# A two-layer hybrid trunk: earlier decays, later masks, softmax scaled on another engine, other durations in the order's model

## The chip, the cores and the metric

One core of a Trainium2 chip runs the whole kernel. The metric is the device time of one execution in microseconds (us). The core's engines each work through a queue of their own in order and wait for each other by semaphores: TensorE (PE) multiplies matrices (PEld is its loading of weights), VectorE (DVE), ScalarE (ACT) and GpSimd (POOL) do the element-wise work, and DMA queues (SP issues most, POOL some) move data.

## The reference

Sequence 256, width 1024, two layers. Each layer is a SwiGLU half-step, a token mixing and a second half-step, each modulated by vectors computed from `c`:

```python
    for l in range(DEPTH):
        mod = c_act @ w_ada[l] + b_ada[l]
        sh1, sc1, gt1, sh2, sc2, gt2, sh3, sc3, gt3 = jnp.split(mod, N_MOD, axis=-1)
        h = modulate(x, ln_ffn1_g[l], sh1, sc1)
        x = x + 0.5 * gt1[:, None, :] * swiglu(h, ffn1_w_gate[l], ffn1_w_up[l], ffn1_w_down[l])
        h = modulate(x, ln_mix_g[l], sh2, sc2)
        x = x + gt2[:, None, :] * token_mixing(h, w_in[l], ...)
        h = modulate(x, ln_ffn2_g[l], sh3, sc3)
        x = x + 0.5 * gt3[:, None, :] * swiglu(h, ffn2_w_gate[l], ffn2_w_up[l], ffn2_w_down[l])
    return rmsnorm(x, final_g)
```

The mixing projects `h` once and gives the columns to three groups, whose outputs are joined and projected back:

```python
    # convolution: GLU, 31 causal taps per channel, LayerNorm, swish
    h = a * jax.nn.sigmoid(gate)
    h = causal_depthwise_conv(h, w_dw) + b_dw
    ...
    # attention (6 heads of 64): softmax over the causal scores, times the values
    p = jax.nn.softmax(jnp.concatenate([s_sel, s_own], axis=-1), axis=-1)
    ...
    # gated delta net (6 heads): short convolution and silu on q, k, v; then per chunk
    g = -jnp.exp(gdn_a_log) * jax.nn.softplus(a + gdn_dt_bias);  beta = jax.nn.sigmoid(b)
    g = jnp.cumsum(g)
    decay = jnp.exp(jnp.where(tril, g[..., :, None] - g[..., None, :], -jnp.inf))
    L = jnp.where(strict, jnp.einsum('bhncd,bhnsd->bhncs', k_beta, k) * decay, 0.0)
    T = lax.linalg.triangular_solve(eye + L, eye, left_side=True, lower=True)
    ...
    # then the state recurrence over the chunks, a gated RMSNorm and silu(z)
```

## The kernel before

The sequence lies in two halves of 128 rows. Weights are split into a high and a low part (`hi` cast on ACT, `lo` subtracted on DVE), and each product of the feed-forward parts and of most of the mixing is made of three matmuls. The phases follow each other: feed-forward, mixing, feed-forward, in each of two layers. The modulation vectors of the coming phases are added up on DVE meanwhile (`adaacc`, `Lb<-raw,c_act`), then summed on PE into bank `px` and reduced to `mod`.

Nobody writes the order of the mixing's instructions out by hand. While the program is built, a class `Clock` keeps a modelled time for each engine and adds `cost(engine, op, ...)` for every instruction. The mixing's side jobs are generators (`sides`): `key_norms`, `query_norms`, `decays`, `pairs`, `gate_conv`, `values_beta`, `inverse`, `delta_rule`, `attention`, two `taps` and `convolution`. Between two products of the main projection, `tick()` steps each generator whose awaited tiles are ready on the modelled clock, or whose named events (`until("kh")`) have been set. On the chip nothing of that model is left but the order in which each engine's instructions stand.

The names that count here. `pm<-Y,raw` are the first, unsplit products of the mixing's projection, `pm<-H,hi` and `pm<-H,lo` the split ones after it, `pm<-hi,H` those of the attention's values. `decays()` makes the exponentials of the decays: `g_g` holds the gates, `pa<-g_g,gt` sums them on PE, `Lb<-kc,g_r` and `S6a<-kc,g_r` spread them on DVE, `PT` takes the exponentials on ACT. `pairs()` multiplies the key products by `PT` into `xin_LT` (called `LD` in the code) and stores its 32x32 diagonal blocks to DRAM (`scr_l`). `inverse()` reads them back as 16x16 blocks (`Lb`), inverts these by 15 steps of two POOL operations (`T<-W,Lb`, `W<-W,T`; "the substitution"), stores the inverses (`scr_w`), reads them back (`Wc`) and joins the blocks on PE (`pa<-Wc,Lb`, `pa<-Lb,Wc` and further steps), the first of them with the off-diagonal blocks `Um` that POOL masks by `Lb<-xin_LT,kc`. `delta_rule()` needs the result. `attention()` makes, for a head, the scores on PE, the row maximum (`mx`) on DVE, the exponential and its sum (`E`, `sm`) on ACT, the reciprocal of the sum on DVE, the scaling of `E` by it, and the transposes `pa<-kc,E` on PE (`turned`), which are copied to `F` and multiplied by the values `V`. A tap of the convolution (`tap`) is either one DVE operation on `cacc`, or a product on ACT into `ctap`, of which there are two buffers, and an addition on POOL (`cacc<-cacc,ctap`); `taps` chooses by the modelled clocks. `closing` ends the mixing and prepares the next phase. All engine calls pass through one helper, so the profile gives the line L171 for each, and a reader goes by the names of the tiles.

Of the kernel before, what the change touches and what calls it, by code (L numbers as in the profile page):

```python
# [13 lines left out]
AF = mybir.ActivationFunctionType  # L14
OP = mybir.AluOpType
# [64 lines left out]
class Clock:  # L80
# [36 lines left out]
    def cost(self, engine, op, out, ins):  # L117
        n = max(self.size(x) for x in [out] + ins[:1])
        if engine == "pe":
            m, n, kind = self.size(ins[0]), self.size(ins[1]), ins[1].dtype  # L120
            if op == "transpose":
                return 0.107
            rows = 4 * max(m, n) if kind == F32 else max(2 * m, n) if kind == F32R else max(64, n)
            return 0.0065 + rows * 0.000435
        if engine == "act":
            return 0.1 + n * 0.00082 if n > 400 else 0.1 + n * 0.0011
        if engine == "gp":
            return max(0.17, 0.08 + n * 0.00222)
        if op == "reciprocal":
            return 0.07 + n * 0.0063  # L130
        return 0.11 + n * 0.00113 if op == "scalar_tensor_tensor" else 0.13 + n * 0.00105
# [46 lines left out]
def trunk(ctx, tc, t, out):  # L178
# [5 lines left out]
    act, dve, pe, gp, sp, qd = (clock.engine(n, e) for n, e in (  # L184
        ("act", nc.scalar), ("dve", nc.vector), ("pe", nc.tensor), ("gp", nc.gpsimd), ("dma", nc.sync), ("dma2", nc.gpsimd)))
# [27 lines left out]
    K = {n: kc[:, o:o + {"tri": 256, "rc": 256, "rs": 256, "eye": 32, "off": 32}.get(n, 128)] for n, o in K_OFF.items() if o < K_RES}  # L213
# [796 lines left out]
    def mixing(l, G, normed, nxt):  # L1010
# [4 lines left out]
        ev = {}  # L1015
# [42 lines left out]
        def until(*names):  # L1058
            while any(n not in ev for n in names):
                yield  # L1060
# [78 lines left out]
        LD = LT[:, :NH * 256].rearrange("p (h t x) -> p h t x", t=2, x=128)  # L1139
# [37 lines left out]
        def key_norms():  # L1177
            yield from until("kconv")

            def back():  # L1180
                act.preload_act_table_set("natural_log_exp_and_others")
                yield from ()

            yield from norms((kh[:, 0:2], kh[:, 2:3]), lambda: act.preload_act_table_set("silu_and_others"), back, 1.0)
            ev["kh"] = True
# [9 lines left out]
            ev["qh"] = True  # L1195

        def decays():
            yield from until("g", "kh")
            g, lnbeta = ev["g"], ev["lnbeta"]
            while any(job[1].tensor.name.startswith("Lb") for job in ada_wait):  # L1200
                extract()
            g, heads = g
            Rs = [sb([128, 1024], tag, F32R).rearrange("p (s k i x) -> p s k i x", s=2, k=2, i=2) for tag in ("Lb", "S6a")]
            cross = sb([128, NH], "g_c")

            def spread(b):
                dve.tensor_tensor(Rs[b % 2].rearrange("p s k i x -> p (s k i) x"), K["tri"][:, 0:128].unsqueeze(1).to_broadcast([128, 8, 128]),
                                  heads[:, 2 * b:2 * b + 2].rearrange("p h k i -> p (h k i)").unsqueeze(2).to_broadcast([128, 8, 128]),
                                  op=OP.mult)

            spread(0)
            spread(1)
            yield from room()
            p = pside([128, NH])
            mm(p, gt.bitcast(F32), g[:, 0], True)
            dve.tensor_tensor(cross, p, lnbeta[:, 0, NH:], op=OP.add)
            for b in range(3):
                R = Rs[b % 2]
                yield (R,)
                yield from room(2)  # L1220
                d = pside([128, 2, 2, 128], True)
                x = pside([128, 2, 128], True)
                for k in range(2):
                    mm(d, gt, R[:, :, k], k == 0, False)
                mm(d, identb, negdb.unsqueeze(1).to_broadcast([128, 4, 128]), False, True)
                for k in range(2):
                    mm(x, onesr, R[:, :, k, 1], k == 0, k == 1)
                if b == 0:
                    spread(2)
                yield (x,)  # L1230
                let_go(d)
                let_go(x)
                for s in range(2):
                    h = 2 * b + s
                    act.activation(PT[:, h, 0:128], d[:, s, 0], AF.Exp, bias=lnbeta[:, 0, NH + h:NH + h + 1])
                    act.activation(PT[:, h, 128:256], x[:, s], AF.Exp, bias=cross[:, h:h + 1])
                    act.activation(PT[:, h, 256:384], d[:, s, 1], AF.Exp, bias=lnbeta[:, 1, NH + h:NH + h + 1])
                    ev["decay", h] = True
            act.preload_act_table_set("silu_and_others")
            ev["silu2"] = True  # L1240

# [125 lines left out]
        def inverse():  # L1367
# [8 lines left out]
            for i in range(2):  # L1376
                c = slice(16 * i, 16 * i + 16)
                qd.dma_start(out=Lb[48 * i:48 * i + 48], in_=scr_l.rearrange("h b j i -> (h b) j i")[:, c, c])
            yield (LD,)
            LM = LD.rearrange("p h t x -> p (h t) x")  # L1380
            for q in QUAD:
                gp.tensor_tensor(Um[q], LM[q, :, q], K["off"][q].unsqueeze(1).to_broadcast([32, 12, 32]), op=OP.mult)
            yield (Lb, W)
            V = W[:, 0]
            for j in range(15):
# [10 lines left out]
            for f in range(2):  # L1396
                for i in range(2):
                    c = slice(16 * i, 16 * i + 16)
                    qd.dma_start(out=scr_w[f].rearrange("h b c i -> (h b) c i")[:, c, c], in_=W[48 * i:48 * i + 48, f])
            for f in (1, 0):  # L1400
                qd.dma_start(out=C[:, f], in_=scr_w[f].rearrange("h b c i -> (b c) h i"))
            yield from until("kh")
# [170 lines left out]
        def attention():  # L1573
# [14 lines left out]
            def softmax(h, p):  # L1588
                yield soon(p)
                mx = sb([128, 2], "mx", bufs=3)  # L1590
                sm = sb([128, 2], "sm", bufs=3)
                P = sb([128, 384], "E", bufs=3)
                for i, c in enumerate(cols):
                    dve.tensor_reduce(mx[:, i:i + 1], p[:, c], axis=AX.X, op=OP.max)
                dve.tensor_scalar(mx, mx, -0.125, None, op0=OP.mult)
                yield (mx,)
                for i, c in enumerate(cols):
                    act.activation(P[:, c], p[:, c], AF.Exp, scale=0.125, bias=mx[:, i:i + 1], accum_out=sm[:, i:i + 1])
                let_go(p)
                yield (sm,)  # L1600
                dve.reciprocal(sm, sm)
                yield (sm,)
                for i, c in enumerate(cols):
                    act.activation(P[:, c], P[:, c], AF.Copy, scale=sm[:, i:i + 1])
                Ps[h] = P
                ev["P", h] = P
                if len(Ps) and h == NH - 1:
                    ev["softmaxed"] = True
# [382 lines left out]
```

## Time and profile before

| what | value |
|---|---|
| time, three runs | 1204.75, 1204.11, 1202.5 us (median 1204.11) |
| the profiled execution: its time, its span | 1202.57 us, 1200.8 us |
| PE, PEld | 1130.7 us (94%), 1052.0 (88%) |
| DVE | 874.4 us (73%) |
| ACT | 612.6 us (51%) |
| POOL | 169.3 us (14%) |
| chain that ended last | PE 71%, DVE 12%, ACT 6%, POOL 6%, issue 3% |
| mean granted TensorE clock | 0.976 |

The span runs from the first to the last instruction of the profiled execution. A share of busy time is an average over phases: the mixings lie at about 235 to 435 us and 817 to 1004 us, the feed-forward parts fill the rest. [...]

### The profile page before, as it was taken

To read this page: it belongs to the slowest core of one execution; us is meant where nothing else is said; L and a number is where in the kernel's file an instruction comes from. 1 tells how busy PE (TensorE), PEld (TensorE's weight loads), DVE (VectorE), ACT (ScalarE), POOL (GpSimd) and SP (SyncE) were. 2 spreads that over 40 slices of the span, in tenths; PEclk is the share of its full clock that TensorE was granted. 3 is DMA by queue.
4 is the path that set the end of the run, shared out by engine and by line. 5 is a ranking of instruction groups with operands and counts; after the bars stand their busy time and mean duration, and the time that the engine had idled before them with its cause. 6 is when DMAs were issued, how large, how long until landed. Compare 5 with 4: busy or idle time off the path is not lost.

```text
span 1200.8 us, 22053 instructions
## 1 busy us (share of the span) xinstructions
PE 1130.7 (94%) x9085; PEld 1052.0 (88%) x9085; DVE 874.4 (73%) x1314; ACT 612.6 (51%) x1049; POOL 169.3 (14%) x213
## 2 busy tenths in 40 slices
PE   5799999999978789999999999999997899999997
PEld 4799999977767789999999999997876789999996
DVE  5778878757965788877778878774886759866554
ACT  4364443548367464434456544444654667544443
POOL 0610000011761010000000000001067401000001
PEclk9899999999999989999999999999999799999999
DMA  8759888836342558969865987892642334876640
GB/s 320 246 186 319 309 299 309 256 113 192 95 137 91 176 176 285 322 243 326 291 218 170 324 313 266 278 300 74 186 140 73 141 108 140 287 257 211 195 139 36
DMA packets 167661, 256.52 MB, mean 214 GB/s; under 512 B 8272, under 2 KB 134056, under 8 KB 167560
## 3 DMA queue, kind: packets, MB, share of 16 engines
q1 hardware_dynamic: 166536, 252.95, 62.6%
q0 software_dynamic: 1024, 2.16, 0.9%
q8 instruction: 71, 1.16, 0.4%
q14 instruction: 30, 0.25, 0.1%
HBM read 252.86 MB, written 2.23 MB: 212 GB/s over the span
## 4 chain that ended last, share of the span: by engine, by line
PE 71%; DVE 12%; ACT 6%; POOL 6%; issue 3%; DMA 1%; SPq 0%; POOLq 0%; DVEq 0%; ACTq 0%
PE pm L171 45%; PE pa L171 25%; DVE lo L171 3%; DVE adaacc L171 3%; PE px L171 2%; ACT hi L171 1%; POOL W L171 1%; POOL cacc L171 1%; POOL T L171 1%; POOL Lb L171 1%; DVE mod L171 1%; ACT L171 1%; DVE tmp L171 1%; DVE Lb L171 1%; DVE Y L171 1%
## 5 line engine op out<-in xcount | busy, mean ns | idle before, releaser
L171 PE MATMUL pm<-H,hi 128*128 128x256 f32 x2816 | 507.7, 283 | 2.8 <-issue 1.6
L171 DVE TENSOR_TENSOR lo<-raw,hi 128x1024 fp32r<-128x1024 f32 (+1 forms) x300 | 362.1, 1226 | 131.8 <-ACT hi L171 131.3
L171 PEld LDWEIGHTS pm<-H,hi 128*128 128x128 f32 x2816 | 431.9, 189 | 5.9 <-issue 2.2
L171 ACT CAST hi<-raw 128x1024 fp32r<-128x1024 f32 (+1 forms) x306 | 311.3, 1040 | 195.3 <-PE pm L171 80.7
L171 PE MATMUL pm<-H,lo 128*128 128x256 f32 x1408 | 392.4, 280 | 1.2 <-DVE lo L171 1.2
L171 PEld LDWEIGHTS pm<-H,lo 128*128 128x128 f32 x1408 | 264.5, 189 | 1.7 <-DVE lo L171 1.6
L171 PE MATMUL pa<-Y,hi 128*128 128x256 f32 x1312 | 241.3, 286 | 4.5 <-DVE xT L171 4.5
L171 PEld LDWEIGHTS pa<-Y,hi 128*128 128x128 f32 x1312 | 204.1, 192 | 6.7 <-DVE xT L171 5.3
L171 PE MATMUL pa<-Y,lo 128*128 128x256 f32 x656 | 185.8, 283 | 0.0
L171 PEld LDWEIGHTS pa<-Y,lo 128*128 128x128 f32 x656 | 127.3, 194 | 0.0
L171 POOL TENSOR_TENSOR xin_LT<-xin_LT 128x256 f32<-128x256 f32 x35 | 27.1, 775 | 664.8 <-ACT xin_LT L171 662.4
L171 ACT CAST Y<-tmp 128x256 fp32r<-128x256 f32 x88 | 35.8, 406 | 131.5 <-DVE tmp L171 131.5
L171 DVE SCALAR_TENSOR_TENSOR adaacc<-raw,c_act,adaacc 128x1024 f32<-128x1024 f32 x70 | 95.5, 1365 | 1.6
L171 DVE SCALAR_TENSOR_TENSOR Lb<-raw,c_act,Lb 128x1024 f32<-128x1024 f32 x56 | 71.8, 1283 | 4.2 <-DMA raw<-in_w_ada_dram 3.0
L171 POOL TENSOR_TENSOR cacc<-cacc,ctap 128x256 f32<-128x256 f32 x54 | 52.3, 973 | 122.0 <-DVE cacc L171 112.8
L171 DVE TENSOR_TENSOR Y<-tmp,Y 128x256 fp32r<-128x256 f32 x88 | 37.4, 425 | 41.5 <-ACT Y L171 41.5
L171 PE MATMUL pm<-Y,raw 128*128 128x256 f32 x288 | 66.8, 384 | 0.0
L171 PEld LDWEIGHTS pm<-Y,raw 128*128 128x128 f32 x288 | 53.4, 190 | 8.9 <-issue 1.0
L171 PE MATMUL pa<-hi,Y 128*128 128x512 f32 x176 | 54.8, 393 | 0.0
L171 ACT ACTIVATE tmp<-pm 128x256 f32<-128x256 f32 x84 | 31.8, 378 | 43.9 <-PE pm L171 43.7
L171 DVE TENSOR_REDUCE mod<-px 128x4 f32<-128x512 f32 x34 | 23.4, 689 | 34.3 <-PE px L171 34.2
L171 DVE SCALAR_TENSOR_TENSOR cacc<-hc,colB,cacc 128x256 f32<-128x256 f32 x66 | 36.0, 562 | 10.3 <-POOL cacc L171 9.4
(309 smaller groups left out, 1342.9 us busy)
## 6 DMA issues: line engine op xcount, KB each, us to landing
raw<-in_w_ada_dram SPq DMA_DIRECT2D x70, 1024.0 KB
raw<-in_ffn_w_gate_dram SPq DMA_DIRECT2D x44, 1024.0 KB
raw<-in_ffn_w_up_dram SPq DMA_DIRECT2D x44, 1024.0 KB
raw<-in_ffn_w_down_dram SPq DMA_DIRECT2D x44, 1024.0 KB
raw<-in_w_in_dram SPq DMA_DIRECT2D x12, 1024.0 KB
raw<-in_w_in_dram SPq DMA_DIRECT2D x20, 512.0 KB
raw<-in_w_out_dram SPq DMA_DIRECT2D x16, 512.0 KB
raw<-in_w_in_dram SPq DMA_DIRECT2D x4, 768.0 KB
```

The source lines that it names most:

```text
L171: return getattr(real, op)(*args, **kw)
```

## The change

Four edits. (1) The durations in `Clock.cost` for ACT and POOL are longer, which changes nothing by itself but the order that the model leads to: of the 60 taps after the first of each half, 27 go through ACT and POOL in each layer before, 13 now, and the others to DVE. (2) `decays()` waits for the event `kconv` (the keys' short convolution) in place of `kh` (the keys' norm), and two later points in it wait for events of the norm (`ktable`, `kh`), which keep the ACT tables in order. (3) The four POOL masks `Lb<-xin_LT,kc` are issued behind the substitution and the `scr_w` stores, ahead of the loads of `Wc`. (4) The scaling of `E` by the reciprocal sums, two operations per head, is a DVE operation in place of an ACT one.

```diff
--- before.py
+++ after.py
@@ -123,9 +123,9 @@
             rows = 4 * max(m, n) if kind == F32 else max(2 * m, n) if kind == F32R else max(64, n)
             return 0.0065 + rows * 0.000435
         if engine == "act":
-            return 0.1 + n * 0.00082 if n > 400 else 0.1 + n * 0.0011
+            return 0.1 + n * 0.00092 if n > 400 else 0.12 + n * 0.0013
         if engine == "gp":
-            return max(0.17, 0.08 + n * 0.00222)
+            return max(0.17, 0.08 + n * 0.0035)
         if op == "reciprocal":
             return 0.07 + n * 0.0063
         return 0.11 + n * 0.00113 if op == "scalar_tensor_tensor" else 0.13 + n * 0.00105
@@ -1179,6 +1179,7 @@
 
             def back():
                 act.preload_act_table_set("natural_log_exp_and_others")
+                ev["ktable"] = True
                 yield from ()
 
             yield from norms((kh[:, 0:2], kh[:, 2:3]), lambda: act.preload_act_table_set("silu_and_others"), back, 1.0)
@@ -1195,7 +1196,7 @@
             ev["qh"] = True
 
         def decays():
-            yield from until("g", "kh")
+            yield from until("g", "kconv")
             g, lnbeta = ev["g"], ev["lnbeta"]
             while any(job[1].tensor.name.startswith("Lb") for job in ada_wait):
                 extract()
@@ -1227,6 +1228,7 @@
                     mm(x, onesr, R[:, :, k, 1], k == 0, k == 1)
                 if b == 0:
                     spread(2)
+                yield from until("ktable")
                 yield (x,)
                 let_go(d)
                 let_go(x)
@@ -1236,6 +1238,7 @@
                     act.activation(PT[:, h, 128:256], x[:, s], AF.Exp, bias=cross[:, h:h + 1])
                     act.activation(PT[:, h, 256:384], d[:, s, 1], AF.Exp, bias=lnbeta[:, 1, NH + h:NH + h + 1])
                     ev["decay", h] = True
+            yield from until("kh")
             act.preload_act_table_set("silu_and_others")
             ev["silu2"] = True
 
@@ -1376,10 +1379,7 @@
             for i in range(2):
                 c = slice(16 * i, 16 * i + 16)
                 qd.dma_start(out=Lb[48 * i:48 * i + 48], in_=scr_l.rearrange("h b j i -> (h b) j i")[:, c, c])
-            yield (LD,)
             LM = LD.rearrange("p h t x -> p (h t) x")
-            for q in QUAD:
-                gp.tensor_tensor(Um[q], LM[q, :, q], K["off"][q].unsqueeze(1).to_broadcast([32, 12, 32]), op=OP.mult)
             yield (Lb, W)
             V = W[:, 0]
             for j in range(15):
@@ -1397,6 +1397,8 @@
                 for i in range(2):
                     c = slice(16 * i, 16 * i + 16)
                     qd.dma_start(out=scr_w[f].rearrange("h b c i -> (h b) c i")[:, c, c], in_=W[48 * i:48 * i + 48, f])
+            for q in QUAD:
+                gp.tensor_tensor(Um[q], LM[q, :, q], K["off"][q].unsqueeze(1).to_broadcast([32, 12, 32]), op=OP.mult)
             for f in (1, 0):
                 qd.dma_start(out=C[:, f], in_=scr_w[f].rearrange("h b c i -> (b c) h i"))
             yield from until("kh")
@@ -1601,7 +1603,7 @@
                 dve.reciprocal(sm, sm)
                 yield (sm,)
                 for i, c in enumerate(cols):
-                    act.activation(P[:, c], P[:, c], AF.Copy, scale=sm[:, i:i + 1])
+                    dve.tensor_scalar(P[:, c], P[:, c], sm[:, i:i + 1], None, op0=OP.mult)
                 Ps[h] = P
                 ev["P", h] = P
                 if len(Ps) and h == NH - 1:
```

With a modelled order, the diff alone doesn't say what moves. Three places follow, in layer 0 (layer 1 is alike). On PE, where the mixing's first products begin, before:

```order
L171 MATMUL pa<-S6a,raw 128x257 x3
L171 MATMUL pa<-Q,raw 128x257
L171 MATMUL pm<-Y,raw 128x256 x16
L171 MATMUL pm<-Y,raw 128x256 x9
L171 MATMUL pa<-tmp,kc 128x512
L171 MATMUL pm<-Y,raw 128x256
L171 MATMUL pa<-tmp,kc 128x256
L171 MATMUL pa<-g_g,gt 128x6
L171 MATMUL pm<-Y,raw 128x256 x6
```

and with the change:

```order
L171 MATMUL pa<-S6a,raw 128x257 x3
L171 MATMUL pa<-Q,raw 128x257
L171 MATMUL pm<-Y,raw 128x256
L171 MATMUL pa<-g_g,gt 128x6
L171 MATMUL pm<-Y,raw 128x256 x15
L171 MATMUL pm<-Y,raw 128x256 x3
L171 MATMUL pa<-tmp,kc 128x512
L171 MATMUL pa<-Lb,gt 128x512 x2
```

The sum of the gates has moved ahead of 25 products, to behind the first; the products with the spread gates (`pa<-Lb,gt`) follow it up. On POOL, from the end of the substitution on, before:

```order
L171 TENSOR_TENSOR cacc<-cacc,ctap 128x256 x4
L171 DMA scr_l<-xin_LT 32x12x32 x4
L171 DMA Lb<-scr_l 48x16x16 x2
L171 TENSOR_TENSOR Lb<-xin_LT,kc 32x384 x4
L171 TENSOR_TENSOR T<-W,Lb 96x15
...
L171 COPY W<-W 96x256
L171 DMA scr_w<-W 48x16x16 x4
L171 DMA Wc<-scr_w 128x12x32 x2
L171 MEMSET S6a 32x12x32
L171 TENSOR_TENSOR cacc<-cacc,ctap 128x256 x23
```

and with the change:

```order
L171 TENSOR_TENSOR cacc<-cacc,ctap 128x256
L171 DMA scr_l<-xin_LT 32x12x32 x4
L171 DMA Lb<-scr_l 48x16x16 x2
L171 TENSOR_TENSOR cacc<-cacc,ctap 128x256
L171 TENSOR_TENSOR T<-W,Lb 96x15
...
L171 COPY W<-W 96x256
L171 DMA scr_w<-W 48x16x16 x4
L171 TENSOR_TENSOR Lb<-xin_LT,kc 32x384 x4
L171 DMA Wc<-scr_w 128x12x32 x2
L171 MEMSET S6a 32x12x32
L171 TENSOR_TENSOR cacc<-cacc,ctap 128x256 x11
```

The masks have moved from ahead of the substitution (the "..." is its other steps) to behind the stores; one tap addition stands ahead of the `scr_l` stores in place of four. On ACT, around the first two heads' scaling, before:

```order
L171 COPY Y<-pm 128x512
L171 ACTIVATE ctap<-hc,colB 128x256 x2
L171 CAST hi<-raw 128x1024 x2
L171 ACTIVATE ctap<-hc,colB 128x256 x2
L171 ACTIVATE E<-E,sm 128x128
L171 ACTIVATE E<-E,sm 128x256
L171 ACTIVATE E<-E,sm 128x128
L171 ACTIVATE E<-E,sm 128x256
L171 ACTIVATE ctap<-hc,colB 128x256 x2
```

and with the change, on DVE:

```order
L171 RECIPROCAL sm<-sm 128x2
L171 TENSOR_REDUCE mx<-pa 128x1 x2
L171 TENSOR_SCALAR mx<-mx 128x2
L171 RECIPROCAL sm<-sm 128x2
L171 SCALAR_TENSOR_TENSOR cacc<-hc,colB,cacc 128x256 x2
L171 TENSOR_SCALAR E<-E,sm 128x128
L171 TENSOR_SCALAR E<-E,sm 128x256
L171 TENSOR_SCALAR E<-E,sm 128x128
L171 TENSOR_SCALAR E<-E,sm 128x256
```

The scaling has left ACT's queue, where casts and taps stood ahead of it, for DVE's, where the two heads' reciprocals, one head's maxima and two taps do.

## Rows read from the trace of the kernel before

**Rows 1.** Busy time of each engine by windows: a feed-forward stretch, a mixing stretch

```profile
core 0: us, PE busy (x) PEld busy (x) DVE busy (x) ACT busy (x) POOL busy (x), PEclk, DMA share, GB/s
80.00:120.00 40.00, 40.00 (x342) 40.00 (x341) 32.53 (x34) 19.63 (x27) 0.00 (x0) 1.00 0.83 287
...
320.00:360.00 40.00, 33.18 (x291) 27.43 (x290) 29.12 (x53) 21.22 (x49) 29.16 (x42) 0.96 0.40 117
```

**Rows 2.** Waits of PE, layer 0 (235:440), then layer 1 (817:1010)

```profile
PE pa L171 <- ACT E L171: 6.7, 4, 4.7
PE px L171 <- DVE mod L171: 4.1, 2, 3.3
PE px L171 <- DVE adaacc L171: 3.8, 1, 3.8
...
PE pa L171 <- ACT V L171: 2.1, 1, 2.1
...
PE pa L171 <- ACT xin_LT L171: 1.0, 1, 1.0
...
PE pa L171 <- ACT E L171: 8.1, 3, 6.4
...
PE pm L171 <- issue: 1.6, 1, 1.6
```

**Rows 3.** Timeline of PE, layer 0: the join, the first transposes of E

```profile
338.17 1.02 PE L171 MATMUL pa<-Wc,Lb 32*32 32x32 f32 x96
...
345.16 1.09 PE L171 MATMUL pa<-kc,E 128*128 128x128 f32 x3 [4.73 <-ACT E L171]
```

**Rows 4.** Timeline of ACT, layer 0, around the softmax

```profile
335.46 0.51 ACT L171 ACTIVATE ctap<-hc,colB 128x256 f32<-128x256 f32 x1 [7.84 <-POOL cacc L171]
...
344.72 1.48 ACT L171 ACTIVATE E<-E,sm 128x128 f32<-128x128 f32 x4
```

**Rows 5.** Timeline of POOL, layer 0, from the first taps to the loads of Wc

```profile
295.63 3.36 POOL L171 TENSOR_TENSOR cacc<-cacc,ctap 128x256 f32<-128x256 f32 x4 [50.91 <-DVE cacc L171]
298.93 2.48 POOL L171 DMA_DIRECT2D scr_l<-xin_LT  x4
305.68 1.46 POOL L171 DMA_DIRECT2D Lb<-scr_l  x2 [4.27 <-PE pa L171]
307.15 4.45 POOL L171 TENSOR_TENSOR Lb<-xin_LT,kc 32x384 f32<-32x384 f32 x4
...
326.77 2.92 POOL L171 DMA_DIRECT2D scr_w<-W  x4
332.26 2.07 POOL L171 DMA_DIRECT2D Wc<-scr_w  x2 [2.56 <-DMA scr_w<-W]
```

**Rows 6.** DMA issues of 290:340 by line, KB each, median us to landing

```profile
Wc<-scr_w POOLq DMA_DIRECT2D x2, 192.0 KB, 4.1
```

**Rows 7.** Windows of half clock (columns as in rows 1)

```profile
345.30:348.70 3.40, 3.38 (x11) 2.60 (x11) 3.37 (x4) 3.40 (x9) 3.02 (x3) 0.50 0.03 5
...
925.60:935.80 10.20, 8.32 (x26) 6.58 (x27) 10.10 (x13) 7.64 (x16) 8.43 (x7) 0.50 0.18 58
...
949.50:959.70 10.20, 10.20 (x84) 8.01 (x85) 7.03 (x18) 4.19 (x13) 0.00 (x0) 0.50 0.01 2
```

**Rows 8.** Timelines of PE and DVE, layer 0, where the mixing's first products begin

```profile
259.08 3.19 PE L171 MATMUL pm<-Y,raw 128*128 128x256 f32 x14
...
261.07 0.17 DVE L171 TENSOR_TENSOR g_g<-g_x,g_ea 128x12 f32<-128x12 f32 x1
```

**Rows 9.** Timelines of DVE and PE, layer 0, at the delta net's values

```profile
296.25 4.36 DVE L171 TENSOR_TENSOR H<-Y,H 128x256 fp32r<-128x256 f32 x8
...
307.56 0.76 PE L171 MATMUL pa<-kc,v 128*128 128x128 f32 x3 [2.01 <-ACT v L171]
```

**Rows 10.** Taps: the page's group on DVE, then timelines of DVE and POOL

```profile
L171 DVE SCALAR_TENSOR_TENSOR cacc<-hc,colB,cacc 128x256 f32<-128x256 f32 x66 | 36.0, 562 | 10.3 <-POOL cacc L171 9.4
...
295.07 0.73 DVE L171 TENSOR_SCALAR cacc<-hc,colB,colA 128x256 f32<-128x256 f32 x2
...
348.80 6.53 POOL L171 TENSOR_TENSOR cacc<-cacc,ctap 128x256 f32<-128x256 f32 x4 [0.16 <-ACT ctap L171]
```

## The prediction

> **What bounds the kernel.** I read the windows first. In the feed-forward stretches TensorE (PE) is busy in every microsecond; in 320 to 360, inside layer 0's mixing, it is busy 33.18 of 40, VectorE (DVE) 29.12, ScalarE (ACT) 21.22, GpSimd (POOL) 29.16 [rows 1]. The 342 matmuls in 40 us also give the price of one PE product, 0.117 us. So the time is PE's work plus what PE waits for in the two mixings, and no other engine is full there. The chain of waits names the waits [rows 2]: in layer 0 the softmax probabilities E (6.7 us, 4.7 of them one wait), the attention values V (2.1), joins (1.0), and at the end the modulation (`mod` 4.1, `adaacc` 3.8); in layer 1, E (8.1, one wait of 6.4) and 1.6 of issue.
>
> Then the timeline behind the long E wait. PE finishes its other work at 345.16 - 4.73 = 340.43 and stands until 345.16 [rows 3]. ACT had stood for 7.84 us until 335.46: its convolution taps have two buffers, and POOL's adds that free them wait behind the substitution. The exponentials thus start late, and the four scalings of E come as late as 344.72, behind casts and more taps, 1.48 us for two heads [rows 4]. So ACT's queue, blocked by POOL, sets PE's largest wait. Finally the clock: after such a wait PE runs for a while at half clock, 0.50 from 345.3 to 348.7 and, in layer 1, for 10.2 us from 925.6 and again from 949.5 [rows 7]. A microsecond waited costs more than itself.
>
> **The change part by part, per layer (layer 0 / layer 1).**
>
> *Decays earlier.* PE meets the cumulative sum `pa<-g_g,gt` behind the first product `pm<-Y,raw`, not behind the 26th. That first product starts at 259.08 and ends 0.44 later, at 259.52; DVE writes `g_g` at 261.07 + 0.17 = 261.24 [rows 8]. The 25 products between, which hid this, now stand behind the sum. With 0.1 for the hand-over PE waits **+1.8 / +1.8**. What DVE does for the decays comes earlier in turn, `xin_LT` is complete some 4 us earlier, and one table load falls away on ACT, which is hidden there.
>
> *Values later.* DVE now does the eight `H<-Y,H` subtractions (4.36) ahead of the value convolutions, since their casts come earlier on ACT. PE already waits 2.01 for the values' silu [rows 9]. By the order I put that silu 3.5 us later; PE itself arrives 1.75 later (1.8 from above, and 3 products more ahead). New wait 3.75, so **+1.75 / +1.75**. Bounds: 0 if the taps that left ACT and POOL let the casts come early enough, +4.4 with the whole of the eight.
>
> *Masks behind the substitution.* Before, POOL issues the scratch stores (`scr_l`) at 298.93 behind four tap adds (3.36), loads Lb at 305.68, multiplies the masks (4.45), substitutes, and issues Wc's loads at 332.26 [rows 5]. Now one add stands ahead instead of four (-2.5; the glu that it needs comes about 0.8 later), so stores start at 297.2, loads at 304.0. With the masks gone the substitution can start when Lb has landed, about 307.2. From the masks' end to the `scr_w` stores is 326.77 - 311.60 = 15.2, so the stores issue at 322.4 to 325.3, the masks run to 329.8, Wc's loads issue to 331.8. They land 4.1 after issue (median, [rows 6]) at about 334, against 336 to 338 before. PE's order has the join earlier too: ahead of it 9 H products, 24 `mv` products and one head of scores fewer, 6.5 us. Join before: 338.17, no wait named [rows 3]. Now 338.17 - 6.5 + 3.2 (the waits above, less the 3 products) = 334.9, or 333.6 where I step row by row. Wait **+0.5 / +0.1**; bounds 0 and 4.45 (the whole of the masks on the path).
>
> *Scaling on DVE, fewer taps on POOL.* The cost table moves 14 of 27 POOL taps per layer to DVE (0.56 each, 7.9 us) and 12 scalings (a 256-wide TENSOR_SCALAR is 0.37; I take 0.37 and 0.25 for 256 and 128, 3.7 us; [rows 10]). Wc's loads are issued at 331.8 against 332.26 + 2.07 = 334.33, so POOL's adds resume 2.5 us earlier, ACT is released near 333.5, its first exponentials come at about 335.6, and DVE has two heads scaled at 341.5. PE arrives at the transposes at 340.43 - 3.2 (27 fewer H products) + 1.7 (the joins' further steps, now ahead, with a 0.7 wait) + 3.2 + 0.3 = 342.4. The wait is gone with 1 us to spare: **-4.7 / -6.4**. With it go the half-clock stretches behind it: 3.4 us at 0.50 are worth 1.7; in layer 1 8.32 us of work in 10.2 are worth 4.2: **-1.7 / -4.2**. Bounds: none of it, if DVE scales as late as ACT did; all.
>
> *Later joins and attention.* The joins all finish ahead of the projection. The smaller waits (E's other three 2.0, V 2.1, joins 1.0; in layer 1 E 1.7 and issue 1.6) shrink to about 1.5 and 1.7: **-3.6 / -1.6**. The half-clock stretch at 949.5 (full 10.2 us busy) follows one of them: **0 / -5.1**. The clock could fall elsewhere: behind the longer wait for the values, which in layer 0 has a slow stretch already, **0 / +1.7**.
>
> *End of the mixing.* PE gets there some 8 us earlier; DVE, which must add up `adaacc` for the next phase and now carries 11.6 us more, does not quite. The waits for `mod` and `adaacc` grow: **+2.1 / +1.0**, an estimate between 0 and 8, since all of PE's gain could be waited away there.
>
> Layer 0: 1.8 + 1.75 + 0.5 - 4.7 - 1.7 - 3.6 + 2.1 = -3.85. Layer 1: 1.8 + 1.75 + 0.1 - 6.4 - 4.2 - 1.6 - 5.1 + 1.7 + 1.0 = -10.95. Sum -14.8 on the profiled execution's 1202.57 (span 1200.8), giving 1187.8. The runs' median, 1204.11, lies 1.5 above that execution; between the two I forecast **1188**. The altered costs in the feed-forward stretches reorder a few casts and subtractions only; PE, full there, hides them.
>
> [...] One POOL row: four tap adds at 348.80 take 6.53, 1.6 each, while DVE runs accumulations; four at 295.63 take 3.36, 0.84 each [rows 5, 10]. [...] DVE is busy beside the substitution before the change as well (29.12 of 40, [rows 1]), so 334 stays in the sum, and a slower POOL is part of the second rival.
>
> **Rivals.**
>
> (a) *Half the gain.* DVE scales 3 us later than I think, behind taps and `lo`, so that a wait of about 2.5 for E remains in each layer, with its half clock. For it: DVE is busy 29 of 40 there, and 11.6 us are added. Then 5 us of wait and 2 to 4 of slow clock come back: 1195 to 1197.
>
> (b) *Slower: the join's loads become the bound.* Wc lands late because the masks' 4.45 now lie between the stores and the loads, and because the one add ahead of `scr_l` still waits for the glu. It decides from where Wc lands behind 338: PE, which arrives at 334 to 335, then waits 4 or more, and with a substitution slowed by a third (5 us) it lands at 339. PE waits 5 and 6.5 in place of the 4.7 and 6.4 for E (+0.4), each with its slow stretch; the 2 x 3.55 of the first two parts and 1.7 of clock stand uncovered, and of the gains only the 5.2 of the later waits is left: 1202.6 + 0.4 + 7.1 + 1.7 - 5.2 = 1206.6. Against it: the store-to-load wait of 2.56 on POOL before [rows 5] is now covered by the masks, so they cost 1.9 net there.
>
> (c) *DVE becomes the bound.* 11.6 us more per layer on 29.12 of 40 would fill it; the taps then end late, the convolution's norm with them, and the projection of its rows waits. PE is held there for as long as DVE is late, some 5 us per layer of the gain: about 1198.
>
> (d) *Nothing.* All that PE gains in the joins is waited away at the closing's `adaacc`; layer 1's clock stretches move but remain: 1202 to 1206.
>
> (e) *More.* Followed row by row, layer 0's mixing ends 11 us earlier, 7 more than the sum of its waits gives, as though waits that the modelled ends of matmuls hide went too. With 7 more there and 3 in layer 1: 1178.
>
> [...]
>
> **How the numbers follow.** The forecast (1183 to 1193) 0.42, (a) 0.14, (c) 0.12, (e) 0.13, (d) 0.07, (b) 0.12. The range from 1173 to 1203 takes in all but (b), most of (d) and the low end of (e). A measurement of this kernel can tell about 0.2%, 2.4 us. Faster: the forecast, (a), (c) and (e), 0.81; same: (d), 0.07; slower: (b), 0.12.
>
> **What would show it.** Right: a wait of 1.5 to 2 for `g_g` near 259.5; a v wait near 3.75; substitution starting within 1 us of 307; Wc read near 334; no E wait over 1 us; PE clock 1.00 after it and less than 10 us of 0.50 per layer. Wrong: PE waiting for Wc, for DVE's E or `cacc`, or the waits for `mod` and `adaacc` grown by the whole gain.

## The result, and the profile after

The changed kernel takes 1187.38 us (median of 4 runs, 1182.18 to 1188.98) where the kernel before took 1203.86 (4 runs). The ratio is 0.9867, interval 0.9845 to 0.9889: 1.3% faster, where 1188 was forecast. The profile's head, with busy time and its share of the span:

```profile
span 1184.1 us, 21996 instructions
## 1 busy us (share of the span) xinstructions
PE 1118.8 (94%) x9085; PEld 1042.9 (88%) x9085; DVE 880.2 (74%) x1354; ACT 596.9 (50%) x1007; POOL 142.0 (12%) x185
```

ACT and POOL have lost the taps and scalings that DVE took over. The mixings by windows, from the first product `pm<-Y,raw` to the next phase, of the kernel before (two lines) and then of the changed one; after the length come busy time by engine and PE's granted clock (1.00 in the feed-forward stretch of [rows 1], 0.50 in the windows of half clock of [rows 7]):

```profile
259.10:434.80 175.70, 152.77 (x1280) 129.55 (x1279) 132.16 (x249) 101.24 (x210) 55.24 (x79) 0.94 0.49 153
840.90:1004.20 163.30, 149.42 (x1272) 126.93 (x1271) 119.39 (x235) 99.80 (x206) 53.90 (x77) 0.94 0.44 136
```

```profile
257.70:427.80 170.10, 148.57 (x1280) 126.91 (x1279) 132.48 (x266) 91.28 (x185) 39.83 (x63) 0.94 0.49 155
831.80:987.90 156.10, 145.89 (x1272) 124.42 (x1271) 122.83 (x255) 91.04 (x185) 40.68 (x63) 0.96 0.46 142
```

Layer 0's mixing is 5.6 us shorter, layer 1's 7.2. PE's idle time in them fell by only 1.4 and 3.7 us (22.9 to 21.5, 13.9 to 10.2); the rest, 4.2 and 3.5, is busy time, for the same 1280 and 1272 matmuls. Part of that is the clock. These are the sums over the windows of half clock inside the two mixings, before and after:

```profile
sum 40.90, PE 37.82; mean PE 5.40
sum 34.30, PE 28.85; mean PE 4.81
```

PE was busy in them for 9.0 us less. In the changed kernel three products `pm<-H` take 0.64 us at 0.50 (from 908.13) and 0.36 at 1.00 (from 911.26); with half of it for the same work at full clock, some 4.5 us came back (an estimate). The other 3.2 us of busy time would be waits inside matmuls whose ends are modelled, as rival (e) had it; that is a reading and not shown. The remaining 3.9 us of the two traces' difference lie outside the mixings: 1.4 ahead of the first, 2.1 in the feed-forward parts between, 0.4 behind the second. I had put nothing there. Over the twelve kernels run below, the first mixing starts anywhere from 257.3 to 259.6 without following an edit, so I don't read a cause into it.

It also matters where in a mixing the gain lies. These windows run from the first product to the first transposes of E, where PE had its longest wait (layer 0 and 1, of the kernel before and then of the changed one; PE's busy time and its clock behind the length):

```profile
259.08:345.16 86.08, 79.25 (x512) 0.98 0.48 140
840.91:927.48 86.57, 77.74 (x512) 0.99 0.47 138
```

```profile
257.68:346.65 88.97, 79.99 (x668) 0.97 0.46 136
831.78:921.96 90.18, 83.27 (x668) 0.92 0.46 133
```

The changed kernel comes to that place 2.9 and 3.6 us later, not earlier, and the work ahead of it is much the same: 168 small matmuls of the joins more, 12 of `pm<-hi,H` and `pm<-lo,H` fewer, about 2 us each. So all that the mixings gain, and more (8.5 and 10.8 us), lies behind the transposes.

The waits of PE, layer 0 and then layer 1, which answer to [rows 2] (total, times, longest):

```profile
PE px L171 <- DVE adaacc L171: 9.5, 2, 5.2
PE pa L171 <- ACT v L171: 4.5, 1, 4.5
PE pa L171 <- issue: 2.8, 1, 2.8
PE pa L171 <- DVE g_g L171: 1.6, 1, 1.6
PE px L171 <- DVE mod L171: 1.6, 2, 0.8
PE pa L171 <- DVE xT L171: 1.5, 1, 1.5
...
PE pa L171 <- ACT v L171: 4.7, 1, 4.7
PE px L171 <- DVE mod L171: 3.0, 1, 3.0
PE pa L171 <- DVE g_g L171: 1.6, 1, 1.6
PE pa L171 <- issue: 0.6, 1, 0.6
PE pa L171 <- DVE xT L171: 0.3, 1, 0.3
```

E, V and the joins are gone from the list. In their place stand `g_g`, a longer `v`, an "issue" inside a join, and in layer 0 more at the closing (`adaacc` and `mod` together 11.1, 7.9 before), where part of what the joins gave is waited away. Three of these lie ahead of the transposes of E: in layer 0 `g_g` 1.6, `v` 2.5 more and "issue" 2.8 make 6.9 us, more than the 4.7 that were waited for E. POOL's timeline, which answers to [rows 5]:

```profile
295.85 0.73 POOL L171 TENSOR_TENSOR cacc<-cacc,ctap 128x256 f32<-128x256 f32 x1 [52.44 <-ACT ctap L171]
296.52 2.48 POOL L171 DMA_DIRECT2D scr_l<-xin_LT  x4
304.03 1.45 POOL L171 DMA_DIRECT2D Lb<-scr_l  x2 [5.03 <-DMA scr_l<-xin_LT]
305.50 0.75 POOL L171 TENSOR_TENSOR cacc<-cacc,ctap 128x256 f32<-128x256 f32 x1
...
322.83 2.92 POOL L171 DMA_DIRECT2D scr_w<-W  x4
325.76 4.36 POOL L171 TENSOR_TENSOR Lb<-xin_LT,kc 32x384 f32<-32x384 f32 x4
330.06 2.09 POOL L171 DMA_DIRECT2D Wc<-scr_w  x2
```

Each of these is within a microsecond of the forecast (stores 297.2, loads 304.0, `scr_w` 322.4, masks to 329.8). Next the timelines of DVE, PE and ACT at the places of [rows 9], [rows 3] and [rows 4]:

```profile
306.28 0.88 DVE L171 SCALAR_TENSOR_TENSOR cacc<-hc,colB,cacc 128x256 f32<-128x256 f32 x2 [2.69 <-POOL cacc L171]
307.07 1.51 DVE L171 SCALAR_TENSOR_TENSOR v<-pm,colB,v 128x255 f32<-128x255 f32 x3
...
340.94 1.00 DVE L171 TENSOR_SCALAR E<-E,sm 128x128 f32<-128x128 f32 x4
...
310.85 0.90 PE L171 MATMUL pa<-kc,v 128*128 128x128 f32 x3 [4.50 <-ACT v L171]
...
334.38 1.01 PE L171 MATMUL pa<-Wc,Lb 32*32 32x32 f32 x96
...
343.32 0.26 PE L171 MATMUL pa<-Wc,Lb 32*32 32x32 f32 x7 [2.79 <-issue]
...
346.65 0.84 PE L171 MATMUL pa<-kc,E 128*128 128x128 f32 x3
...
333.52 0.51 ACT L171 ACTIVATE ctap<-hc,colB 128x256 f32<-128x256 f32 x1 [6.10 <-POOL cacc L171]
...
335.76 0.35 ACT L171 ACTIVATE E<-pa,mx 128x128 f32<-128x128 f32 x1
```

Two things to see. DVE's last value convolutions start late because a tap ahead of them waits 2.69 us for a POOL add (305.50), and that add stands behind the loads of Lb, which POOL issues only when the scratch stores have landed (5.03 us of waiting ahead of 304.03). And ACT is still blocked on its tap buffers, for 6.10 us, only until 333.52 in place of 335.46.

### The profile page after: what moved, and what is told of

Same layout as the page of the kernel before. It is cut to its first block, busy times and chain, and to the rows that moved or that the text cites. A ratio compares the mean times of both kernels' runs of the same rounds, so it can differ in the third digit from the quotient of the medians.

```text
span 1184.1 us, 21996 instructions
## 1 busy us (share of the span) xinstructions
PE 1118.8 (94%) x9085; PEld 1042.9 (88%) x9085; DVE 880.2 (74%) x1354; ACT 596.9 (50%) x1007; POOL 142.0 (12%) x185
## 3 DMA queue, kind: packets, MB, share of 16 engines
HBM read 252.86 MB, written 2.23 MB: 215 GB/s over the span
## 5 line engine op out<-in xcount | busy, mean ns | idle before, releaser
L171 PE MATMUL pa<-Y,hi 128*128 128x256 f32 x1312 | 235.3, 283 | 3.5 <-DVE xT L171 2.7
L171 PEld LDWEIGHTS pa<-Y,hi 128*128 128x128 f32 x1312 | 201.6, 190 | 4.7 <-DVE xT L171 3.5
L171 DVE SCALAR_TENSOR_TENSOR cacc<-hc,colB,cacc 128x256 f32<-128x256 f32 x94 | 47.9, 528 | 8.0 <-POOL cacc L171 6.8
L171 POOL TENSOR_TENSOR cacc<-cacc,ctap 128x256 f32<-128x256 f32 x26 | 26.0, 1010 | 131.0 <-ACT ctap L171 126.0
```

Of the source, the lines that this page charges most:

```text
L171: return getattr(real, op)(*args, **kw)
```

## The experiments

The working theory was the forecast's: the scaling of E left a queue in which it stood late. It is **A** below; its rival **B** is that the places decide, whatever the engine. In all ratios the kernel before ran on the same chip.

**One part alone.** Four kernels take one hunk of the diff each. The softmax hunk:

```diff
-                    act.activation(P[:, c], P[:, c], AF.Copy, scale=sm[:, i:i + 1])
+                    dve.tensor_scalar(P[:, c], P[:, c], sm[:, i:i + 1], None, op0=OP.mult)
```

> Only the softmax scaling goes to DVE. Theory A (the scalings stood late because they were in ACT's queue): the wait of PE for E falls from 4.7 and 6.4 us to under 1.5, the half clock behind it goes, about 1190 to 1194 us. Rival B (the place in the order decides, not the engine): by the order DVE now has a rotation, two sums of adaacc (3.4) and two subtractions lo (3.5) ahead of the first scaling, so PE still waits 4 us or more for E, now put down to DVE, and the time is 1200 to 1208 us.

Measured: 1209.84 us, ratio 1.0072 (1.0052 to 1.0093): slower. DVE's timeline:

```profile
347.59 3.41 DVE L171 SCALAR_TENSOR_TENSOR adaacc<-raw,c_act,adaacc 128x1024 f32<-128x1024 f32 x2
350.93 3.41 DVE L171 TENSOR_TENSOR lo<-raw,hi 128x1024 fp32r<-128x1024 f32 x2
354.26 1.95 DVE L171 TENSOR_SCALAR E<-E,sm 128x128 f32<-128x128 f32 x4
```

The scaling moved from 344.72 [rows 4] to 354.26. PE's wait moved on to `lo` (8.6 and 9.5 us) and not, as B had it, to E (0.5): in this order it meets products that need those two subtractions ahead of E's transposes. The time lies above B's range too. Theory A falls: another engine alone doesn't bring the scaling forward.

The masks' hunk:

```diff
-            yield (LD,)
-            for q in QUAD:
-                gp.tensor_tensor(Um[q], LM[q, :, q], ...)
...
+            for q in QUAD:
+                gp.tensor_tensor(Um[q], LM[q, :, q], ...)
             for f in (1, 0):
                 qd.dma_start(out=C[:, f], ...)
```

> Only the masks move behind the substitution. The scalings stay on ACT but stand behind the exponentials in the order, casts behind them. Theory A: the wait for E stays above 3 us, about 1200 us. Rival B: it falls below 1 us in both layers, and half or more of the gain is there, 1188 to 1196 us, with no wait for g_g and 2 us for the values.

Measured: 1206.96, ratio 1.0053 (1.0029 to 1.0078). The wait for E is gone (0.4 us in layer 0), as B had it, and still the kernel is slower: `v` is waited for 6.5 and 6.2 us, and by windows PE's clock is 0.88 and 0.90 in its two mixings, against 0.94 before. Neither theory foresaw that. By these rows the loss is the clock's: PE's idle time in the two mixings is 33.9 us, 36.8 before, but in the windows of half clock PE is busy for 69.2 us, 37.8 before, and half of that difference, what it costs by estimate, is 15.7 us. Why the clock falls so much more here is not shown.

```profile
257.50:437.30 179.80, 157.40 (x1280) 134.93 (x1279) 134.62 (x257) 98.04 (x203) 43.97 (x69) 0.88 0.46 149
845.10:1010.00 164.90, 153.37 (x1273) 130.95 (x1273) 122.83 (x242) 96.24 (x198) 40.98 (x66) 0.90 0.43 135
...
sum 77.80, PE 69.18; mean PE 7.69
```

The decays' hunk:

```diff
-            yield from until("g", "kh")
+            yield from until("g", "kconv")
...
+                yield from until("ktable")
...
+            yield from until("kh")
```

> Only the decays wait for the convolution. Both theories: 1.6 us of wait for g_g and 4.5 for the values per layer. Here the join stands behind 114 H products in place of 144, ahead of the mv products, and the masks ahead of the substitution: PE arrives near 332 and waits 2 to 5 us for Wc; the scalings on ACT stand behind six taps and a cast, so by A and by B a wait for E remains unless the join's wait covers it. 1198 to 1206 us.

Measured: 1201.31, ratio 1.0013 (0.9995 to 1.0031). Waits of 1.6 for `g_g` and 4.2 for `v` as expected; the wait for Wc that was expected is not named, and those for E are 0.8 and 0.7. In layer 0 what that gives is spent at the end (`adaacc` 8.8) and on `g_g` and `v`: its named waits add up to 23.5 us, 23.6 before.

The durations' hunk:

```diff
-            return 0.1 + n * 0.00082 if n > 400 else 0.1 + n * 0.0011
+            return 0.1 + n * 0.00092 if n > 400 else 0.12 + n * 0.0013
-            return max(0.17, 0.08 + n * 0.00222)
+            return max(0.17, 0.08 + n * 0.0035)
```

> Only the durations in the order's model change (19 taps through POOL in place of 27, scalings on ACT behind two casts of 1024 and two taps). If the four parts were worth a sum of their own, this one would have to bring all of the gain and the losses of the others, -25 us or more: below 1180. If the places in the order decide, PE meets the transposes of E with 30 mv products and no join ahead, the scalings are as late as before, a wait for E of 3 to 6 us stays per layer, and the time is 1198 to 1206 us.

Measured: 1182.49, ratio 0.9842 (0.9826 to 0.9859). The expectation missed: this hunk, which changes only the order and which engine takes a tap (19 of the taps go through POOL in each layer, 27 before), gives all of the gain by itself. The four ratios alone add up to -0.2%, the four together give -1.3%: they don't add. ACT's timeline shows what I had overlooked:

```profile
328.04 0.59 ACT L171 COPY Y<-pm 128x512 f32<-128x512 f32 x1 [11.49 <-PE pm L171]
...
329.26 0.37 ACT L171 ACTIVATE E<-pa,mx 128x128 f32<-128x128 f32 x1
...
336.67 1.49 ACT L171 ACTIVATE E<-E,sm 128x128 f32<-128x128 f32 x4
```

No tap that must wait for POOL stands ahead of the exponentials, so ACT isn't blocked behind the substitution. The exponentials come at 329.26, the scalings at 336.67, eight us before [rows 4], on ACT and still behind two casts and two taps. Of E, 2.9 us are waited for in layer 0, at later heads; `v` costs 5.1. At the end of the mixing `mod` and `adaacc` cost 1.3 in place of 7.9, but `Y` costs 5.2 there.

**One part left out.** The changed kernel with one hunk undone (the hunks above reversed).

```diff
-                    dve.tensor_scalar(P[:, c], P[:, c], sm[:, i:i + 1], None, op0=OP.mult)
+                    act.activation(P[:, c], P[:, c], AF.Copy, scale=sm[:, i:i + 1])
```

> The change without its softmax part: the scaling is back on ACT, where by the order it stands directly behind the exponentials and one copy, with no casts between. Theory A: the wait for E comes back with 3 us or more per layer, 1195 to 1200 us. Rival B: no wait for E over 1 us, and the time is within 0.3% of the changed kernel's, 1184 to 1191 us.

Measured: 1187.83, ratio 0.9887 (0.9866 to 0.9908): the time of the changed kernel, with no wait for E in the list. ACT scales at 339.88. In the changed kernel the softmax part is worth nothing that these runs can tell.

```diff
-            return max(0.17, 0.08 + n * 0.0035)
+            return max(0.17, 0.08 + n * 0.00222)
```

(and ACT's line likewise)

> The change without the new durations: 22 taps through POOL, the join stands behind 102 H products in place of 135, the transposes of E ahead of all mv products. If the places decide, PE arrives at the join about 331 and at E some 3 us sooner than ACT and DVE can have it: waits of 2 to 4 us for Wc or E per layer, and the time is 1194 to 1202 us. If the durations only matter through the taps' load, no wait for Wc and 1186 to 1192 us.

Measured: 1203.31, ratio 1.0018 (1.0004 to 1.0031): without the durations nothing is left, and the time lies above both ranges. The forms of the waits missed: beside `adaacc` (8.9 in layer 0) and "issue" they are small, with 17 us at half clock in a row in layer 1. The wait for E is short although ACT is blocked here for 7.54 us and once more for 2.23, and the scalings come later than in the kernel before; the rows are DVE's and PE's:

```profile
346.96 1.00 DVE L171 TENSOR_SCALAR E<-E,sm 128x128 f32<-128x128 f32 x4
...
347.39 0.61 PE L171 MATMUL pa<-kc,E 128*128 128x128 f32 x3 [1.13 <-DVE E L171]
```

PE itself comes late, as in the changed kernel (88.7 us behind the first product).

```diff
-            yield from until("g", "kconv")
+            yield from until("g", "kh")
```

(and the two later waits taken out)

> The change without the earlier decays: no wait for g_g, 2 us for the values. By the order DVE scales E behind a rotation, two sums of adaacc and two lo, as in the run with the softmax part alone, so that run's wait of 8 to 9 us for lo comes back and the time is 1200 to 1210 us. If the earlier decays were only a cost (1.6 for g_g and 2.5 more for the values per layer), it would be faster than the changed kernel, about 1179.

Measured: 1192.17, ratio 0.9908 (0.9885 to 0.993). The expectation missed on both sides: no long wait for `lo` (2.0, 1.5), and a `v` of 4.2 without the earlier decays, so those don't make it.

```diff
             LM = LD.rearrange("p h t x -> p (h t) x")
+            for q in QUAD:
+                gp.tensor_tensor(Um[q], LM[q, :, q], ...)
```

(and taken out ahead of Wc's loads)

> The change with the masks again ahead of the substitution: waits of 1.6 for g_g and 4.5 for the values stay; the join stands behind 24 mv products more, the transposes of E behind 171 H and 48 mv products, so no wait for Wc or E; closing waits for adaacc and mod as in the changed kernel. If the moved masks are not needed 1185 to 1191 us; if the substitution's later end (4.4 us) is felt, waits in the later joins and 1193 to 1199 us.

Measured: 1202.62, ratio 1.0007 (0.9996 to 1.0019). The time lies above both ranges. PE waits 7.2 us for `lo` in each layer; `v` fell to 1.7, not foreseen.

**The block by itself.** The kernel before with the order of every engine kept, and nine taps per layer skipped:

```diff
+                slow[0] += 1
+                if 7 <= slow[0] <= 15:
+                    m = slow[-2]
+                    slow.append(m)
+                    clock.tile("ctap", 2, m)
+                    clock.note("act", "activation", (m, hc[:, b, k:k + S], AF.Copy), dict(scale=w))
+                    clock.note("gp", "tensor_tensor", (ca[:, b], ca[:, b], m), {})
+                else:
                     m = sb([128, S], "ctap", bufs=2)
```

> The kernel before, every instruction in its place, but without nine of the 62 taps of each layer's convolution (the 7th to 15th of those through ACT and POOL, which are left out of the sum). Theory (ACT is blocked on its tap buffers behind the substitution, so the exponentials and scalings of E come late): ACT's wait of 7.84 and 9.89 us is gone, the exponentials come near 330 in place of 337.5, the waits of 4.7 and 6.4 for E fall below 1, and with their slow clock the time is 1184 to 1193 us. Rival (the scalings are late because they stand behind casts on ACT): a wait of 2.5 us or more for E stays in each layer, 1195 us or more.

Measured: 1185.48, ratio 0.9874 (0.9851 to 0.9898). ACT's timeline and what is left of E in the waits of layer 0:

```profile
325.46 0.58 ACT L171 COPY Y<-pm 128x512 f32<-128x512 f32 x1 [11.07 <-PE pm L171]
...
327.07 0.37 ACT L171 ACTIVATE E<-pa,mx 128x128 f32<-128x128 f32 x1
...
337.22 1.49 ACT L171 ACTIVATE E<-E,sm 128x128 f32<-128x128 f32 x4
```

```profile
PE pa L171 <- ACT E L171: 0.5, 2, 0.3
```

With the block gone the wait for E is gone (1.9 is left in layer 1), though the scalings stand where they stood, behind the casts. Nine taps taken off ACT and POOL, engines that were busy for 51% and 14% of the span, are worth as much as the whole change. So the block is what made E late in the kernel before, and taking it away is enough to win that time. It is not shown that the changed kernel wins by the same: the equal ratios come from different parts. In the mixings this kernel takes 13.3 us off PE's idle time and 1.4 off its busy time, the change 5.1 and 7.7. The skipped adds also leave POOL with less to do, which may help DVE (its busy time falls by 2.2 us in each mixing; see the last section); that isn't separated here. The number of adds left doesn't decide alone: with 16 and 19 per layer (masks alone, decays alone) nothing is gained, with 19 and 23 (durations alone, decays left out) there is a gain.

**The wait for the values.** The changed kernel with no tap through POOL while the substitution is being planned:

```diff
-                    tap(b, left[b] == CONVK or clock.t["dve"] <= clock.t["pe"] + AHEAD)
+                    tap(b, left[b] == CONVK or not cfg["lo_pool"] or clock.t["dve"] <= clock.t["pe"] + AHEAD)
```

> The changed kernel, with no tap through POOL while the substitution is being planned, so that no add stands behind the loads of Lb. Theory (the longer wait for the values is DVE standing for that one add): the wait for v falls from 4.5 to 2 us or less in both layers and the time by 3 to 6 us, to 1181 to 1185. Rival (the forecast's reason, the eight H subtractions ahead of the value convolutions, which stay where they are): v stays above 3.5 and the time at 1186 to 1189.

Measured: 1189.23, ratio 0.9912 (0.9889 to 0.9935). The wait for `v` is 1.7 in both layers, so its cause is settled: the add behind the loads. But no time is gained, against 1181 to 1185 expected, and the list of layer 0 says where it went:

```profile
PE pa L171 <- DMA Wc<-scr_w: 5.1, 1, 5.1
```

Layer 1 has the same 5.1. PE comes to the join earlier and waits for Wc, whose loads POOL issues at 330.66. In the changed kernel, the wait for `v` had covered that one.

**Two more orders.** The durations alone with the same edit to the taps:

```diff
+            return max(0.17, 0.08 + n * 0.0035)
...
+                    tap(b, left[b] == CONVK or not cfg["lo_pool"] or clock.t["dve"] <= clock.t["pe"] + AHEAD)
```

> The new durations alone, with the same edit to the taps: wait for v from 5.1 to about 2 us, the join behind all mv products as in the run with the durations alone; 1176 to 1181 us if nothing else opens. Rival: the taps that DVE takes over make its casts and rotations late, and the wait moves to lo or E: 1182 to 1190.

Measured: 1185.61, ratio 0.9885 (0.9855 to 0.9915). `v` is off the list. In layer 0 `mod` 5.4 and 23.9 us at half clock in a row are new, `Y` still costs 3.5: the rival's time, though its waits (`lo`, E) are not the ones. And POOL's duration alone:

```diff
-            return max(0.17, 0.08 + n * 0.00222)
+            return max(0.17, 0.08 + n * 0.0035)
```

> Only POOL's new duration in the order's model, ACT's as before. By the order three adds stand ahead of the stores, none behind the loads of Lb, and the first exponentials stand ahead of the tap that is blocked. Theory: this figure is what frees ACT: no long wait for E, 2 us for v, 1180 to 1188 us. Rival (ACT's durations do it, or both are needed): a wait for E of 3 us or more and 1196 us or more.

Measured: 1188.96, ratio 0.9921 (0.9894 to 0.9949). The long wait for E is gone (1.5 and 0.9 in all), by this one figure; about half of the gain of both durations is there, and the time is 1 us above the range. `mod` takes 7.0 in layer 0.

The fastest of all these is the durations alone. Its interval (0.9826 to 0.9859) overlaps that of the whole change (0.9845 to 0.9889) a little, so that it is as fast is shown, that it is faster is likely.

## Why the prediction was right

The time and its sign came out; the terms did so less evenly, and in part by luck (layer 0 / layer 1, forecast, then measured).

- *Decays earlier*, +1.8 / +1.8: 1.6 / 1.6. Right.
- *Values later*, +1.75 / +1.75: 2.5 / 2.7 (4.5 and 4.7 less the 2.0 of before). Of the named step the cause was wrong. The eight subtractions took 2.76 us, not 4.36, and are not what `v` waits for; it is the tap's add behind POOL's loads. The order shown ahead of the prediction has that add; I gave it no price.
- *Masks behind the substitution*, join +0.5 / +0.1: no wait at 334.38, with POOL's times as forecast. But rival (b) is nearer than its 0.12: taking the `v` wait away uncovered 5.1 us for Wc. The forecast's arrival at the join (334.9) has the `v` wait in it; without that wait PE would have stood here instead, so the two terms depend on each other and the later of the two arrivals counts.
- *Scaling on DVE, fewer taps on POOL*, -4.7 / -6.4: both waits are gone, exponentials at 335.76 (335.6 forecast), scalings done at 341.94 (341.5). But the place where PE had waited is not reached earlier: PE meets the transposes at 346.65, not at 342.4, held up by `g_g`, `v` and "issue", so E has 4.7 us to spare and not 1. E as late as before, 86.1 us behind the first product, would have been in time as well, for PE comes 89.0 behind it. So either would do in this kernel, an earlier E (shown in the order before by skipping nine taps) or a later PE (shown by the change without the durations, where E is late and the wait 1.13), and the 4.7 and 6.4 are not time won: the waits ahead, in layer 1 with two stretches of half clock, took their place. Of the two reasons given, the engine is not one: with the scaling back on ACT the time is the same, and alone it makes the kernel slower.
- *Slow clock*, -1.7 / -7.6 (4.2 + 5.1 - 1.7): half of what fell away of PE's busy time at half clock is 1.5 / 3.0, so layer 0 is right in size and layer 1 is not. Half clock lasts 20.5 us in layer 0 as before and 13.7 in layer 1, 20.5 before, where less than 10 per layer was the sign of being right. That each new wait brings a slow stretch of its own, which would give the 1193 at the top of the forecast's band, no run shows: behind the new waits for `g_g` (1.6) the clock stays at 1.00 to 310.3 and 883.8, and behind those for `v` (4.5 and 4.7) it is 0.50 for 3.4 us in layer 0, as long as before the change, and for 6.8 in layer 1. In layer 1 both stretches lie ahead of the transposes now (883.9 to 890.7, 904.3 to 911.2), the first at the new wait for `v`; before, both began at E's wait or later. In layer 0 a stretch still covers the transposes (344.5 to 348.0, 345.3 to 348.7 before), now behind the "issue" of 2.79.
- *Later joins and attention*, -3.6 / -1.6: E's others, V and the joins are off the list, 5.1 and more; but 2.8 and 0.6 of "issue" in a join are new. Net -2.3 / -2.7, right in sum.
- *End of the mixing*, +2.1 / +1.0: in layer 0 `adaacc` and `mod` 11.1 against 7.9, less a shorter `xT`; in layer 1 `mod` 3.0, new. Right in kind, DVE's sum for the next phase is what PE meets next, and that is why gains in the joins of layer 0 come through only in part.
- *DVE's load*, 11.6 more per layer in that term and in rivals (a) and (c): by windows its busy time in the mixings grew by 0.3 / 3.4, for the operations it had already got shorter. Its taps (`cacc<-hc,colB,cacc`) took 562 ns in the mean [rows 10] and now take 528; the eight H subtractions took 4.36 [rows 9], with POOL's adds of 295.63 to 298.99 [rows 5] beside them, and now 2.76 from 297.69, with no add beside them.

So the sum of -14.8 stands beside -16.7 of span with errors of both signs in it. Layer 1 was to give 11.0 and gave 7.2, layer 0 3.85 and gave 5.6, and 3.9 lie where I had put nothing. By kind, the named waits were to give 5.5 and PE's idle time gave 5.1, which is right; the clock was to give 9.3 and gave some 4.5. That 3.2 us of busy time and 3.9 outside the mixings, neither of them in the sum, fill the hole is luck.

What stays open: why each of three parts alone is no gain, or a loss, is shown by waits run by run (and by the clock for the masks), but not as one cause; each changes the place of hundreds of instructions. Which of the moved instructions bring the 8.5 and 10.8 us behind the transposes is not shown. The 3.9 us outside the mixings are not explained.

## What to carry to other kernels

Where a model orders the instructions, a truer duration in it can be worth more than the edits to the work: here a ratio of 0.9842 alone, against 1.0013 to 1.0072 for each of the others (the model had a POOL add at 0.65 us and now has 0.98; the trace of the kernel before has 0.97 in the mean). And the edits didn't add up, -0.2% as a sum and -1.3% together: run each alone and each left out before giving one the credit. ACT, which feeds POOL's adds through two buffers, stood for 7.84 us here [rows 4], for the adds that free them stood behind POOL's substitution, stores and loads [rows 5], and the exponentials stood behind ACT's blocked tap; look for such a block first when a short operation comes late. And when a wait is to be taken away, ask which later wait it covers: with the wait for `v` down from 4.5 to 1.7 us PE waited 5.1 for Wc, which had not been in the list, and the time was no shorter (1189.23 against 1187.38). A wait that is gone from the list is not yet time won: count from the start of the phase to the place where it stood.

## What the hardware showed besides

The same operations of DVE and POOL took longer side by side: the four scalings of E take 1.00 us while POOL is idle (340.94 above) and 1.95 while POOL works through nine adds without a pause, which take 11.73, or 1.30 each, against 0.75 for the lone one at 305.50 above, while DVE stands (run with the softmax part alone):

```profile
344.14 11.73 POOL L171 TENSOR_TENSOR cacc<-cacc,ctap 128x256 f32<-128x256 f32 x9 [1.34 <-ACT ctap L171]
```

Both sides are slower here; the trace doesn't show by what.

In the middle of 96 matmuls of 32x32, with 89 of them done, PE stood for 2.79 us and nothing in the profile released it (the row at 343.32); in layer 1 it was 0.57 with 74 done. Ten of the twelve other kernels have "issue" in their lists of waits too, 0.4 to 4.2 us a row. One thing goes with it: within that stand the trace has one packet of the queue q8, whose kind the profile gives as `instruction`.

```profile
q8 instruction: 1, 0.02, 2.3%
```

It lasts from 340.91 to 341.92, and PE goes on 1.4 us after its end. The whole trace has 71 of these packets for PE's 18170 matmuls and weight loads, one for 256 of them if all are PE's. The only other stands in the mixings of the two kernels that nothing releases end alike: a packet from 916.97 to 917.85 and PE at 919.43, 1.6 us later (the changed kernel, layer 1), a packet from 947.1 to 948.1 and PE at 949.40, 1.3 us later (the kernel before). So my reading is that PE waits there for its next instructions; no run was made to test it.
